# Six of the weight ring's units become three double-width tiles, loaded from weights laid out in pairs of experts

## The chip, the cores and the metric

One core of one Trainium2 chip runs the whole program in one launch. The metric is the device time of that launch in microseconds. Before the change it is 1020.64 us (median of 3 runs, 1019.25 to 1020.99).

## The reference

Two transformer layers run one after the other on 256 tokens of width 1024. The first has a mixer (differential attention and gated linear attention), a cross attention to a memory, and a mixture of experts; the second has three attention branches, one of them a cross attention to the same kind of memory. All is float32. The part that matters here is the mixture of experts: 32 experts, two per token, each with three matrices.

```python
def expert_block(args):                       # N_EXPERTS = 32, D_MODEL = 1024, D_EXPERT = 512
    xb, e = args
    hid = jax.nn.silu(xb @ w_gate[e]) * (xb @ w_up[e])     # w_gate, w_up: 32 x 1024 x 512
    return hid @ w_down[e]                                 # w_down:        32 x 512 x 1024
...
kv = rmsnorm(mem, g_mem) @ w_mem_kv           # second layer: 1024 x 1024, the memory's keys and values
```

## The kernel before

The mixture of experts works on groups of four experts (q = 0 to 7), each expert with 32 token slots, so that four experts fill the 128 columns of TensorE. `experts(q)` gathers the tokens, multiplies by gate and up (L1065), forms the hidden rows, multiplies by down (L1090) and adds the result to the tokens (L1101, L1108).

Every weight is loaded once. A "unit" is 8 KB on each of 128 partitions, 1024 KB, and one unit holds half of one matrix of one expert: 192 units in all, 24 per q, asked for four at a time by `weights(4)` (one for each of the four experts). Units live in a ring of 20 slots. The string `ORDER = "222222uuuu11111uuu3u"` says, request by request, from which pool the slot comes: `2` from `ring2` (tag w2, 6 slots), `u` from `utp` (tag ut, 8 slots shared with other tiles), `1` from `ring1` (w1, 5 slots), `3` from `ring3` (w3, one slot). `unit()` (L89) takes the letter at `st["n"]` and steps on. A slot is written again when the instructions that read what it held are done; the wait for it stands on the load itself.

All weight loads are issued by SyncE's queue (SP), which is in order: a load that waits holds back all behind it. Loads take one of eight completion semaphores in turn, so a load also waits for the one eight places before it. The first 20 requests are chained in program order (`chained()`, L1000); later a scheduler places them.

Beside the experts stands work for the second layer, as filler: after q = 4 `mem2_k` (L1179) and after q = 5 `mem2_v` multiply the normalised memory by `w_mem_kv_2`. Each asks for two units through `w_units` (L146, its load is L156), which calls the same `unit()`; so these two requests take the next two letters of the ring. `mem2_k` is the 121st and 122nd request, letters 1 and 2 of the string's seventh turn. Each of its units is split chunk by chunk into a high and a low part, on ScalarE (`whf`, L327) and VectorE (`wlf`, L328), with two buffers of each, and each chunk feeds 12 matmuls (L363, L365, L366).

`pack()` on the host prepares the inputs; `woven` puts the rows of an expert's matrix in the order in which a partition wants them, so that a unit is 1024 KB in one piece in HBM.

Of the kernel before, what the change touches and what calls it, by code (L numbers as in the profile page):

```python
# [8 lines left out]
F32 = mybir.dt.float32  # L9
# [7 lines left out]
P = 128  # L17
# [51 lines left out]
def tile_layers(ctx: ExitStack, tc: tile.TileContext, A, out, dbg=None, upto=99):  # L69
    nc = tc.nc  # L70
    V, S, PE, G, SP = nc.vector, nc.scalar, nc.tensor, nc.gpsimd, nc.sync
    R1, R2, R3, UT, K2A, K2B = 5, 6, 1, 8, 26, 31
# [12 lines left out]
    st = {"ring2": None, "n": 0, "floor": 10 ** 9}  # L85

    ORDER = "222222uuuu11111uuu3u"

    def unit(dt=F32):  # L89

        if st["ring2"] is None:
            return ring1.tile([P, 2048], dt, tag="w1", name="w1", bufs=R1)
        r = ORDER[st["n"] % len(ORDER)]
        st["n"] += 1
        if r == "u":
            return ut((P, 2048), dt)
        if r == "1":
            return ring1.tile([P, 2048], dt, tag="w1", name="w1", bufs=R1)
        if r == "2":
            return st["ring2"].tile([P, 2048], dt, tag="w2", name="w2", bufs=R2)  # L100
        return st["ring3"].tile([P, 2048], dt, tag="w3", name="w3", bufs=R3)

    def pad(pool, nbytes):

        G.memset(pool.tile([P, nbytes // 4], F32, name="pad")[:, :1], 0.0)
# [7 lines left out]
    def tiny(n, dt=F32):  # L113
        return small.tile([P, n], dt, tag=f"t{n}", name=f"t{n}", bufs=8 if n < 32 else 3)

    def k2(shape=(P, 512), dt=F32):
        return st["k2"].tile(list(shape), dt, tag="k2", name="k2")

    def ut(shape=(P, 2048), dt=F32, name="ut"):
        return utp.tile(list(shape), dt, tag="ut", name=name, bufs=UT)  # L120
# [25 lines left out]
    def w_units(W, c0, n, k0, nd, dmas=1, before=None):  # L146

        us = []
        for k in range(k0, k0 + nd, 4):
            u = unit()  # L150
            v = u[:, :4 * n].rearrange("p (d n) -> p d n", d=4)
            c = 4 // dmas
            for i in range(0, 4, c):
                if before:
                    before(k + i, c)
                SP.dma_start(v[:, i:i + c], W[(k + i) * P:(k + i + c) * P, c0:c0 + n].rearrange("(d p) n -> p d n", p=P))  # L156
            us.append(v)
        return us
# [12 lines left out]
    def load_T(t, src):  # L171
        return lambda d, n: SP.dma_start(t[:, d:d + n], src[:, d * T:(d + n) * T].rearrange("p (d t) -> p d t", d=n))

    us = w_units(A["w_in"], 0, 512, 0, 8, 2, load_T(xT, A["xT"]))
# [525 lines left out]
    for tt in range(2):  # L700
# [7 lines left out]
        for hp in range(2):  # L708
            for cc in range(2):
                c = 2 * tt + cc  # L710
# [31 lines left out]
    for tt in range(2):  # L742
        t = k2()
# [75 lines left out]
    for hp in range(2):  # L819
        for tt in range(2):  # L820
# [9 lines left out]
            for hh in range(2):  # L830
                j = 2 * hp + hh
# [9 lines left out]
    for hd in range(4):  # L841
# [4 lines left out]
        p = wspf.tile([P, 2, T], F32, tag="whf", name="p", bufs=2)  # L846
# [151 lines left out]
    loads, loaded = [], []  # L998

    def chained():  # L1000

        return tc.issue_after(st["dma"].ins) if 0 < len(loaded) < len(ORDER) else nullcontext()

    def add_gu(q, k):
        def go(g, j):
            u = unit().rearrange("p (d n) -> p d n", d=4)
            with chained():
                st["dma"] = SP.dma_start(u, A[g][4 * q + j, 4 * k * P:(4 * k + 4) * P, :].rearrange("(p d) n -> p d n", p=P))
            return [u]
        loads.extend([lambda g=g, j=j: go(g, j) for g in ("w_e_gate", "w_e_up") for j in range(4)])  # L1010

    def add_dn(q, k, fine):
        W = A["w_e_down"]

        def go(j):
            u = unit().rearrange("p (c n) -> p c n", c=2)
            with chained():
                st["dma"] = SP.dma_start(u, W[4 * q + j, 2 * k * P:2 * (k + 1) * P, :].rearrange("(p c) n -> p c n", p=P))
            return [u]

        def go_fine():
            us = [unit().rearrange("p (c n) -> p c n", c=2) for _ in range(4)]
            for b, c0, c1 in ((0, 0, 2), (1, 0, 1), (1, 1, 2)):
                for j in range(4):
                    SP.dma_start(us[j][:, c0:c1, b * 512:(b + 1) * 512],
                                 W[4 * q + j, 2 * k * P:2 * (k + 1) * P, b * 512:(b + 1) * 512]
                                 .rearrange("(p c) n -> p c n", p=P)[:, c0:c1])
            return us
        loads.extend([go_fine] if fine else [lambda j=j: go(j) for j in range(4)])

    for q in range(8):
        for k in range(2):
            add_gu(q, k)
        for k in range(2):
            add_dn(q, k, fine=q == 7 and k == 1)
# [222 lines left out]
    for tt in range(2):  # L1258
# [5 lines left out]
        w = tiny(8)  # L1264
# [8 lines left out]
    for tt in range(2):  # L1273
        nk = (tt + 1) * P
        acc = accs[tt]
        for p0 in range(0, 4, 4 // (tt + 1)):
            n = 4 // (tt + 1)
# [6 lines left out]
            for r in range(2):  # L1284
                rl = k2((P, n, nk))
                S.activation(rl, pss[r], AF.Relu)
                for p in range(n):
                    g = 2 * (p0 + p) + r
# [154 lines left out]
    for tt in range(2):  # L1443
        m4, s4, nb, r4 = tiny(4), tiny(4), tiny(4), tiny(4)
        for f in range(2):
# [7 lines left out]
            for hh in range(2):  # L1453
                j = 2 * f + hh
                S.activation(x[:, hh], ps[:, hh], AF.Exp, bias=nb[:, j:j + 1], scale=isc, accum_out=s4[:, j:j + 1])
            V.reciprocal(r4[:, c2], s4[:, c2])
            for hh in range(2):
                j = 2 * f + hh
# [3 lines left out]
    for hd in range(4):  # L1462
# [4 lines left out]
        p = k2((P, 2, T))  # L1467
# [35 lines left out]
def pack(inputs):  # L1503
    f = {k: np.asarray(v) for k, v in inputs.items()}
    c, m = shape_constants()
    row = lambda *n: [f[k].reshape(-1) for k in n]
    vecs = np.concatenate(row("norm_mix", "norm_cross", "norm_mem", "norm_ffn", "g_in_2", "g_mem_2", "b_merge_2",
                              "da_q_norm", "da_q_norm", "da_k_norm", "da_k_norm", "da_out_norm", "gla_out_norm",
                              "cross_q_norm", "cross_k_norm")).reshape(NVEC, P)

    woven = lambda w, c: w.reshape(32, -1, c, P, w.shape[-1]).transpose(0, 1, 3, 2, 4).reshape(w.shape)
    chunks = lambda w: np.ascontiguousarray(w.reshape(8, P, -1).transpose(1, 0, 2).reshape(P, -1))
    feature = lambda x: x.T.reshape(8, P, T).transpose(1, 0, 2).reshape(P, -1)
    a = {
        "x": f["x"][0], "mem": f["mem"][0], "mem_2": f["mem_2"][0],
        "xT": feature(f["x"][0]), "memT": feature(f["mem"][0]), "vecT": vecs.T, "cst": c, "cstm": m,
        "lam": np.concatenate([f[k] for k in ("lambda_q1", "lambda_k1", "lambda_q2", "lambda_k2")], 0),
        "gw": np.tile(np.pad(f["gla_gate_w"][0], ((0, 16), (0, 0))), (4, 1)), "gb": f["gla_gate_b"],
        "w_gr": chunks(np.pad(f["w_in"][0][:, 3072:3088], ((0, 0), (0, 16)))),
        "w_rt": chunks(np.concatenate([f["w_group"][0], np.zeros((D, 4), np.float32), f["w_expert"][0]], 1)),  # L1520
        "b_rt": np.concatenate([f["b_group"][0], np.full(4, -3e38, np.float32), f["b_expert"][0]])[None],
        "g_final": f["g_final_2"][None],
    }
    for k in ("w_in", "w_o", "w_cq", "w_ckv", "w_co", "w_e_gate", "w_e_up", "w_e_down", "w_in_2", "w_mem_kv_2",
              "w_up_moba_2", "w_up_dsa_2", "w_up_cross_2", "w_out_2"):
        a[k] = f[k][0]
    for k, c in (("w_e_gate", 4), ("w_e_up", 4), ("w_e_down", 2)):
        a[k] = woven(a[k], c)
    return {k: np.ascontiguousarray(v) for k, v in a.items()}


_INS = ("x", "mem", "mem_2", "xT", "memT", "vecT", "cst", "cstm", "lam", "gw", "gb", "w_gr", "w_rt", "b_rt", "g_final",
        "w_in", "w_o", "w_cq", "w_ckv", "w_co", "w_e_gate", "w_e_up", "w_e_down", "w_in_2", "w_mem_kv_2",
        "w_up_moba_2", "w_up_dsa_2", "w_up_cross_2", "w_out_2")


# [14 lines left out]
```

## Time and profile before

| | us |
|---|---|
| median of 3 runs | 1020.64 |
| the profiled execution, its own time | 1020.82 |
| its span, on which all times below are read | 1019.2 |
| TensorE busy | 905.2 (89%) |
| VectorE, ScalarE busy | 445.4, 357.8 |
| data read from HBM | 292.98 MB |
| chain that ended last: TensorE, DMA | 46%, 40% |

The times of the rows are microseconds from the span's start. The span is cut into 40 slices of 25.5 us on the page; the mixture of experts lies in slices 11 to 28, counted from 1 (about 255 to 712 us). GB/s is what the core's 16 DMA engines moved. In a row of time, a bracket holds the idle time before the instruction and what ended it. A wait of the queue is read as the time between two issues.

### The profile page before, as it was taken

To read this page: it belongs to the slowest core of one execution; us is meant where nothing else is said; L and a number is where in the kernel's file an instruction comes from. 1 tells how busy PE (TensorE), PEld (TensorE's weight loads), DVE (VectorE), ACT (ScalarE), POOL (GpSimd) and SP (SyncE) were. 2 spreads that over 40 slices of the span, in tenths; PEclk is the share of its full clock that TensorE was granted. 3 is DMA by queue.
4 is the path that set the end of the run, shared out by engine and by line. 5 is a ranking of instruction groups with operands and counts; after the bars stand their busy time and mean duration, and the time that the engine had idled before them with its cause. 6 is when DMAs were issued, how large, how long until landed. Compare 5 with 4: busy or idle time off the path is not lost.

```text
span 1019.2 us, 14146 instructions
## 1 busy us (share of the span) xinstructions
PE 905.2 (89%) x5611; PEld 603.0 (59%) x5611; DVE 445.4 (44%) x999; ACT 357.8 (35%) x687; POOL 48.0 (5%) x180
## 2 busy tenths in 40 slices
PE   6999999999978869678797897778999999999996
PEld 6787788877423313114152251113878788999994
DVE  4596664535311202003030130103997967646465
ACT  5675765444101001002020020003645656554443
POOL 1101423101000001000000000000000000000000
PEclk9999999999989999899899999979999999999998
DMA  9853354698899999999999999999645352446531
GB/s 328 317 165 125 125 172 159 212 388 316 358 420 426 426 427 426 429 426 427 426 422 426 424 426 426 428 427 338 209 149 180 105 186 84 143 153 200 187 124 42
DMA packets 77029, 294.98 MB, mean 289 GB/s; under 512 B 5280, under 2 KB 8096, under 8 KB 52768
## 3 DMA queue, kind: packets, MB, share of 16 engines
q1 hardware_dynamic: 76672, 293.48, 74.0%
q8 instruction: 45, 0.74, 0.3%
q10 hardware_dynamic: 288, 0.57, 0.1%
q14 instruction: 24, 0.20, 0.1%
HBM read 292.98 MB, written 1.05 MB: 288 GB/s over the span
## 4 chain that ended last, share of the span: by engine, by line
PE 46%; DMA 40%; DVE 6%; ACT 4%; POOL 2%; issue 1%; DVEq 0%; SPq 0%; ACTq 0%; POOLq 0%
DMA ut<-w_e_up 15%; DMA w<-w_e_up 10%; DMA ut<-w_e_down 7%; PE mm L357 6%; PE mm L363 6%; PE mm L365 6%; PE mm L366 6%; PE mm L358 6%; PE mm L356 6%; DMA w<-w_e_down 5%; DVE wlm L328 2%; DMA ut<-w_mem_kv 2%; PE mm L1065 2%; ACT whm L327 1%; PE mm L1090 1%
## 5 line engine op out<-in xcount | busy, mean ns | idle before, releaser
L328 DVE TENSOR_TENSOR wlm<-w,whm 128x1024 fp32r<-128x1024 f32 (+3 forms) x144 | 168.5, 1173 | 110.3 <-ACT whm L327 108.7
L327 ACT ACTIVATE whm<-w 128x1024 fp32r<-128x1024 f32 (+3 forms) x144 | 145.6, 1014 | 145.1 <-PE mm L365 69.8
L1065 PE MATMUL mm<-w,xg 128*32 128x512 f32 x616 | 148.0, 661 | 33.3 <-DMA w<-w_e_gate 18.5
L363 PE MATMUL mm<-uh,whm 128*128 128x256 f32 x448 | 129.1, 288 | 6.6 <-ACT whm L327 6.6
L365 PE MATMUL mm<-ul,whm 128*128 128x256 f32 x448 | 128.3, 286 | 0.0
L1065 PE MATMUL mm<-ut,xg 128*32 128x512 f32 x408 | 108.0, 643 | 22.8 <-DMA ut<-w_e_up 15.4
L366 PE MATMUL mm<-uh,wlm 128*128 128x256 f32 x448 | 128.0, 286 | 0.0
L357 PE MATMUL mm<-wlm,uh 128*128 128x512 f32 (+2 forms) x288 | 111.4, 387 | 4.0 <-DVE wlm L328 4.0
L356 PE MATMUL mm<-whm,uh 128*128 128x512 f32 (+2 forms) x288 | 110.7, 388 | 0.4 <-ACT uh L291 0.2
L358 PE MATMUL mm<-whm,ul 128*128 128x512 f32 (+2 forms) x288 | 110.7, 385 | 0.0
L1090 PE MATMUL mm<-w,hT 128*32 128x512 f32 x320 | 83.8, 599 | 12.4 <-DMA w<-w_e_down 9.7
L363 PEld LDWEIGHTS mm<-uh,whm 128*128 128x128 f32 x448 | 86.9, 194 | 7.4 <-ACT whm L327 6.6
L1065 PEld LDWEIGHTS mm<-w,xg 128*32 128x32 f32 x616 | 32.0, 119 | 93.6 <-issue 44.5
L365 PEld LDWEIGHTS mm<-ul,whm 128*128 128x128 f32 x448 | 87.0, 194 | 0.6 <-issue 0.2
L366 PEld LDWEIGHTS mm<-uh,wlm 128*128 128x128 f32 x448 | 86.9, 194 | 0.1
L1065 PEld LDWEIGHTS mm<-ut,xg 128*32 128x32 f32 x408 | 24.8, 116 | 75.9 <-issue 30.8
L1090 PE MATMUL mm<-ut,hT 128*32 128x512 f32 x192 | 58.8, 599 | 7.4 <-DMA ut<-w_e_down 5.7
L357 PEld LDWEIGHTS mm<-wlm,uh 128*128 128x128 f32 x288 | 54.2, 188 | 17.2 <-DVE wlm L328 7.4
L356 PEld LDWEIGHTS mm<-whm,uh 128*128 128x128 f32 x288 | 53.8, 188 | 11.0 <-ACT whm L327 0.9
L358 PEld LDWEIGHTS mm<-whm,ul 128*128 128x128 f32 x288 | 54.1, 188 | 10.1 <-issue 0.3
L1097 DVE COPY eo<-mm 128x256 f32<-128x256 f32 x16 | 6.8, 424 | 119.1 <-ACT eo L1096 119.1
L1053 DVE SCALAR_TENSOR_TENSOR mt<-mt,mm 128x512 f32<-128x512 f32 x8 | 5.5, 687 | 119.2 <-ACT mt L1052 119.2
(349 smaller groups left out, 1261.4 us busy)
## 6 DMA issues: line engine op xcount, KB each, us to landing
w<-w_in SPq DMA_DIRECT2D x42, 1024.0 KB, 4.9
w<-w_e_gate SPq DMA_DIRECT2D x42, 1024.0 KB, 19.6
w<-w_e_down SPq DMA_DIRECT2D x37, 1024.0 KB, 19.6
w<-w_e_up SPq DMA_DIRECT2D x35, 1024.0 KB, 19.6
ut<-w_e_up SPq DMA_DIRECT2D x29, 1024.0 KB, 19.5
ut<-w_e_down SPq DMA_DIRECT2D x23, 1024.0 KB, 19.6
ut<-w_e_gate SPq DMA_DIRECT2D x22, 1024.0 KB, 19.5
w<-w_ckv SPq DMA_DIRECT2D x8, 1024.0 KB, 5.1
```

The source lines that it names most:

```text
L327: S.activation(wh, src, AF.Copy)
L328: st["wl"] = V.tensor_tensor(wl, src, wh.bitcast(F32), op=OP.subtract)
L356: PE.matmul(o, uh[:, d, sl], wh[:, dd], start=d == d0, stop=False)
L357: PE.matmul(o, uh[:, d, sl], wl[:, dd], start=False, stop=False)
L358: PE.matmul(o, ul[:, d, sl], wh[:, dd], start=False, stop=d == d1)
L363: PE.matmul(o, wh[:, dd, sl], uh[:, d], start=d == d0 and f % 2 == 0, stop=False, skip_group_check=True)
L365: PE.matmul(o, wh[:, dd, sl], ul[:, d], start=False, stop=False, skip_group_check=True)
L366: PE.matmul(o, wl[:, dd, sl], uh[:, d], start=False, stop=d == d1, skip_group_check=True)
L1053: V.scalar_tensor_tensor(t, t, 1.0, gp, op0=OP.add, op1=OP.mult)
L1065: PE.matmul(ps[32 * j:32 * j + 32], xg[:, d, 32 * j:32 * j + 32], us[j][:, dd], start=d == 0, stop=d == 7, tile_position=(0, 32 * j))
L1090: PE.matmul(dn[b][32 * j:32 * j + 32], hT[:, c, 32 * j:32 * j + 32], us[j][:, cc, b * 512:(b + 1) * 512], start=c == 0, stop=c == 3, tile_ ...
L1097: V.tensor_copy(o[:, 256:], dn[b][:, 256:])
```

## The change

`unit_pair()` is new: where the next two letters are both `2`, it takes one tile of 16 KB per partition (tag w2, 3 of them in the same room) and gives its two halves; elsewhere it gives two single units. The host lays the same half matrix of two neighbouring experts side by side: a row of 4096 floats per partition, 16 KB, of which the first 8 KB belong to one expert and the second to the next. A double tile is loaded by one transfer of 2048 KB; single units are loaded by one transfer each, of half of every such row. The very last group of loads (`go_fine`) and the overflow path read the old arrays. The branch for letter `2` in `unit()` is gone; a single request that meets that letter takes the last line, `ring3`.

```diff
         if r == "1":
             return ring1.tile([P, 2048], dt, tag="w1", name="w1", bufs=R1)
-        if r == "2":
-            return st["ring2"].tile([P, 2048], dt, tag="w2", name="w2", bufs=R2)
         return st["ring3"].tile([P, 2048], dt, tag="w3", name="w3", bufs=R3)
+
+    def unit_pair():
+
+        if ORDER[st["n"] % len(ORDER)] + ORDER[(st["n"] + 1) % len(ORDER)] == "22":
+            st["n"] += 2
+            t = st["ring2"].tile([P, 4096], F32, tag="w2", name="w2", bufs=R2 // 2)
+            return t, [t[:, :2048], t[:, 2048:]]
+        return None, [unit(), unit()]
...
+    def go(src):
+        t, us = unit_pair()
+        for u, w in [(t, src)] if t is not None else zip(us, (src[:, :2048], src[:, 2048:])):
+            with chained():
+                st["dma"] = SP.dma_start(u, w)
+        return us
+
     def add_gu(q, k):
-        def go(g, j):
-            u = unit().rearrange("p (d n) -> p d n", d=4)
-            with chained():
-                st["dma"] = SP.dma_start(u, A[g][4 * q + j, 4 * k * P:(4 * k + 4) * P, :].rearrange("(p d) n -> p d n", p=P))
-            return [u]
-        loads.extend([lambda g=g, j=j: go(g, j) for g in ("w_e_gate", "w_e_up") for j in range(4)])
+        loads.extend([lambda g=g, j=j: [u.rearrange("p (d n) -> p d n", d=4) for u in go(A[g][2 * q + j, k])]
+                      for g in ("w_gate_2", "w_up_2") for j in range(2)])
...
+
+        a[k.replace("_e", "") + "_2"] = a[k].reshape(16, 2, 2, P, 2048).transpose(0, 2, 3, 1, 4).reshape(16, 2, P, 4096)
```

SP's queue at the end of q = 4, before the change. `w2_3981` and `w2_3983` are the two units of `mem2_k`, `w3_3940` is a unit of q = 4's down matrices, and what follows is q = 5's gate.

```order
L1018 DMA w3_3940<-w_e_down 128x2048
L1018 DMA ut_3942<-w_e_down 128x2048
L156 DMA w2_3981<-w_mem_kv_2 128x4x512
L156 DMA w2_3983<-w_mem_kv_2 128x4x512
L1008 DMA w2_4117<-w_e_gate 128x2048
L1008 DMA w2_4119<-w_e_gate 128x2048
L1008 DMA w2_4121<-w_e_gate 128x2048
L1008 DMA w2_4123<-w_e_gate 128x2048
```

The same place of SP's queue in the changed kernel:

```order
L1014 DMA w3_3904<-w_down_2 128x2048
L1014 DMA ut_3905<-w_down_2 128x2048
L1014 DMA w2_4081<-w_gate_2 128x4096
L162 DMA w3_3945<-w_mem_kv_2 128x4x512
L1014 DMA w2_4083<-w_gate_2 128x4096
L1014 DMA w1_4143<-w_gate_2 128x2048
L162 DMA w3_3947<-w_mem_kv_2 128x4x512
L1014 DMA w1_4144<-w_gate_2 128x2048
L1014 DMA w1_4147<-w_gate_2 128x2048
```

The memory's two units now carry the tag w3, as the unit of q = 4 two places ahead does, and they stand behind and between loads of q = 5, with three units of q = 5 between them. They are the only single units of the program that meet letter `2`.

ScalarE's order around `mem2_k`, before (`eo` is the end of q = 4, `whf` the split of the memory's weights, `xg` the gather for q = 6, `mt` the hidden rows of q = 5):

```order
L1096 ACTIVATE eo_3969<-mm_3911 128x256
L327 ACTIVATE whf_3985<-w2_3981 128x512
L327 ACTIVATE whf_4001<-w2_3981 128x512
L327 ACTIVATE whf_4017<-w2_3981 128x512
L327 ACTIVATE whf_4033<-w2_3981 128x512
L327 ACTIVATE whf_4049<-w2_3983 128x512
```

and in the changed kernel:

```order
L1100 ACTIVATE eo_3933<-mm_3875 128x256
L968 ACTIVATE xg_4128<-sm_4129,vec_86 128x128
L968 ACTIVATE xg_4128<-sm_4136,vec_86 128x128
L968 ACTIVATE xg_4128<-sm_4191,vec_86 128x128
L333 ACTIVATE whf_3949<-w3_3945 128x512
L333 ACTIVATE whf_3965<-w3_3945 128x512
L968 ACTIVATE xg_4128<-sm_4198,vec_86 128x128
L333 ACTIVATE whf_3981<-w3_3945 128x512
```

The gather for q = 6 moved ahead of the split; on TensorE it moved likewise, and the first two matmuls of q = 5's gate units moved in between. Elsewhere the three engines keep their order but for two matmuls that changed places.

SP's queue where the ring turns for the first time, before (`w2_2816` is the 21st request, the first that takes a used slot of the ring):

```order
L1018 DMA w3_2665<-w_e_down 128x2048
L1018 DMA ut_2667<-w_e_down 128x2048
L1018 DMA w2_2816<-w_e_down 128x2048
L1018 DMA w2_2818<-w_e_down 128x2048
L1018 DMA w2_2820<-w_e_down 128x2048
L1018 DMA w2_2822<-w_e_down 128x2048
```

and in the changed kernel:

```order
L1014 DMA w3_2659<-w_down_2 128x2048
L1014 DMA ut_2660<-w_down_2 128x2048
L1014 DMA w2_2810<-w_down_2 128x4096
L1014 DMA w2_2812<-w_down_2 128x4096
L1014 DMA w2_2848<-w_gate_2 128x4096
```

Two loads stand where four stood, each behind the readers of both units that the slot held. There are 29 such loads in the program, 3 of them in the first 20 requests; 130 single units remain, 116 of them behind the first 20 requests.

## Rows read from the trace of the kernel before

**Rows 1.** The page: DMA share (tenths) and GB/s in 40 slices

```profile
DMA  9853354698899999999999999999645352446531
GB/s 328 317 165 125 125 172 159 212 388 316 358 420 426 426 427 426 429 426 427 426 422 426 424 426 426 428 427 338 209 149 180 105 186 84 143 153 200 187 124 42
```

**Rows 2.** Engines by stretch; after the engines: PEclk, DMA share, GB/s

```profile
255.00:262.00 7.00, 6.63 (x56) 3.14 (x56) 2.79 (x16) 0.73 (x2) 0.00 (x0) 1.00 0.62 260
262.00:264.00 2.00, 2.00 (x18) 1.64 (x15) 0.35 (x1) 0.05 (x1) 0.00 (x0) 1.00 0.68 143
264.00:266.00 2.00, 2.00 (x20) 0.77 (x22) 0.68 (x2) 0.68 (x2) 0.00 (x0) 1.00 0.93 393
266.00:268.00 2.00, 2.00 (x21) 0.48 (x13) 0.00 (x0) 0.00 (x0) 0.00 (x0) 1.00 1.06 442
420.00:460.00 40.00, 29.27 (x132) 7.01 (x132) 2.52 (x6) 1.58 (x3) 0.00 (x0) 0.91 1.01 427
```

**Rows 3.** Chain of waits in order of time: start, us, what

```profile
257.52 0.89 PE mm L1065 x2
...
263.71 12.09 DMA w<-w_e_down
...
564.55 19.78 DMA ut<-w_mem_kv
...
584.39 19.56 DMA ut<-w_e_up
...
698.85 1.48 PE mm L1090 x9
```

**Rows 4.** The page: DMA issues, count, KB each, us to landing

```profile
w<-w_e_gate SPq DMA_DIRECT2D x42, 1024.0 KB, 19.6
...
w<-w_co SPq DMA_DIRECT2D x4, 1024.0 KB, 5.0
```

**Rows 5.** SP's queue in time, end of q = 4 and after

```profile
493.16 0.33 SPq L1018 DMA_DIRECT2D w<-w_e_down  x1
495.63 0.33 SPq L1018 DMA_DIRECT2D ut<-w_e_down  x1
...
535.10 12.75 SPq L1008 DMA_DIRECT2D ut<-w_e_up  x3
```

**Rows 6.** TensorE in time at the end of q = 4

```profile
512.81 1.90 PE L1090 MATMUL mm<-w,hT 128*32 128x512 f32 x4 [0.54 <-DMA w<-w_e_down]
515.25 0.64 PE L1090 MATMUL mm<-ut,hT 128*32 128x512 f32 x3 [0.53 <-DMA ut<-w_e_down]
...
516.99 1.88 PE L1090 MATMUL mm<-ut,hT 128*32 128x512 f32 x4
...
522.14 0.68 PE L363 MATMUL mm<-uh,whf 128*128 128x256 f32 x1
```

**Rows 7.** ScalarE in time at the end of q = 4

```profile
518.11 0.38 ACT L1096 ACTIVATE eo<-mm 128x256 f32<-128x256 f32 x1 [16.74 <-PE mm L1090]
```

**Rows 8.** VectorE in time at the end of q = 4

```profile
522.23 1.28 DVE L1108 TENSOR_TENSOR h<-sm,h 128x512 f32<-128x512 f32 x2
...
526.21 0.69 DVE L328 TENSOR_TENSOR wlf<-w,whf 128x512 fp32r<-128x512 f32 x1 [0.81 <-ACT whf L327]
```

**Rows 9.** SP's queue in time, first fill and first turn of the ring

```profile
198.14 0.34 SPq L1008 DMA_DIRECT2D w<-w_e_gate  x1
...
251.54 0.33 SPq L1018 DMA_DIRECT2D ut<-w_e_down  x1
261.67 0.33 SPq L1018 DMA_DIRECT2D w<-w_e_down  x1
...
262.45 1.17 SPq L1018 DMA_DIRECT2D w<-w_e_down  x2
```

**Rows 10.** TensorE in time, the end of q = 5's filler and after

```profile
533.98 0.28 PE L366 MATMUL mm<-uh,wlf 128*128 128x256 f32 x1
...
549.84 3.63 PE L1065 MATMUL mm<-w,xg 128*32 128x512 f32 x28 [1.45 <-DMA w<-w_e_gate]
```

More of the change, by code (lines that the diff above doesn't have):

```diff
@@ L1002, in chained @@
         return tc.issue_after(st["dma"].ins) if 0 < len(loaded) < len(ORDER) else nullcontext()
-    def add_gu(q, k):
-        def go(g, j):
-            u = unit().rearrange("p (d n) -> p d n", d=4)
-            with chained():
-                st["dma"] = SP.dma_start(u, A[g][4 * q + j, 4 * k * P:(4 * k + 4) * P, :].rearrange("(p d) n -> p d n", p=P))
-            return [u]
-        loads.extend([lambda g=g, j=j: go(g, j) for g in ("w_e_gate", "w_e_up") for j in range(4)])
+    def go(src):
[4 more added lines that the diff above has]
+        return us
+    def add_gu(q, k):
+        loads.extend([lambda g=g, j=j: [u.rearrange("p (d n) -> p d n", d=4) for u in go(A[g][2 * q + j, k])]
+                      for g in ("w_gate_2", "w_up_2") for j in range(2)])
     def add_dn(q, k, fine):
         W = A["w_e_down"]
[L1015 to L1019, printed above, removed]
         def go_fine():
-            us = [unit().rearrange("p (c n) -> p c n", c=2) for _ in range(4)]
+            us = [u.rearrange("p (c n) -> p c n", c=2) for _ in range(2) for u in unit_pair()[1]]
             for b, c0, c1 in ((0, 0, 2), (1, 0, 1), (1, 1, 2)):
@@ L1028, in go_fine @@
             return us
-        loads.extend([go_fine] if fine else [lambda j=j: go(j) for j in range(4)])
+        loads.extend([go_fine] if fine else [lambda j=j: [u.rearrange("p (c n) -> p c n", c=2) for u in go(A["w_down_2"][2 * q + j, k])]
+                                             for j in range(2)])
     for q in range(8):
@@ L1528, in pack @@
         a[k] = woven(a[k], c)
+        a[k.replace("_e", "") + "_2"] = a[k].reshape(16, 2, 2, P, 2048).transpose(0, 2, 3, 1, 4).reshape(16, 2, P, 4096)
     return {k: np.ascontiguousarray(v) for k, v in a.items()}
 _INS = ("x", "mem", "mem_2", "xT", "memT", "vecT", "cst", "cstm", "lam", "gw", "gb", "w_gr", "w_rt", "b_rt", "g_final",
-        "w_in", "w_o", "w_cq", "w_ckv", "w_co", "w_e_gate", "w_e_up", "w_e_down", "w_in_2", "w_mem_kv_2",
-        "w_up_moba_2", "w_up_dsa_2", "w_up_cross_2", "w_out_2")
+        "w_in", "w_o", "w_cq", "w_ckv", "w_co", "w_e_gate", "w_e_up", "w_e_down", "w_gate_2", "w_up_2", "w_down_2", "w_in_2",
+        "w_mem_kv_2", "w_up_moba_2", "w_up_dsa_2", "w_up_cross_2", "w_out_2")
 def kernel(**inputs):
```

## The prediction

> **What bounds the kernel now.** I read the slices of the page first. From slice 12 on, for sixteen slices, the 16 DMA engines are busy throughout and move 420 to 429 GB/s; the last twelve slices have 42 to 209 [rows 1]. This is the mixture of experts, and TensorE is not what holds it: in the 40 us from 420 it is busy for 29 [rows 2]. The chain of waits says the same: from 263.71 on it is almost only DMA, in links of mostly 19.56 us, up to the last down group at 698.85 [rows 3]. A link is one load from issue to landing, 19.6 us against 5.0 for a load that finds the queue empty [rows 4]. Eight loads are in flight, so a unit lands every 19.56/8 = 2.445 us (1.0486 MB in that time is 428.9 GB/s). In this stage every microsecond in which the DMA engines have nothing to do comes out at the end, and what TensorE does costs nothing unless it holds back a load.
>
> **Part 1, the wide loads themselves.** 29 loads of 2048 KB replace 58 of 1024; 26 of them lie behind the first turn of the ring, where DMA bounds. What is a row worth that is 16 KB long instead of 8? The link that holds `mem2_v`'s two units took 19.78 against 19.56 for one without [rows 3]. Those units come in rows of 2 KB, 32 rows per engine and unit instead of 8, so 48 more rows per engine cost 0.22 us, 4.6 ns a row. A wide load saves 8 rows per engine, 37 ns; 26 of them save 1.0 us. The row's own cost may not fall if the engines cut 16 KB in pieces: then 0. On the other side, the quickest stretch shown is 442 GB/s [rows 2]; wide loads at that rate instead of 428.9 would save 3% of 26 x 4.89 us, 3.8 us. I take -1.0, the value of the nearest row, with 0 and -3.8 as ends.
>
> **Part 2, the single units.** Their rows stay 8 KB long but now lie 16 KB apart. Before shows no such load. The nearest are the memory's units, 2 KB rows 4 KB apart, and 0.11 us a unit is all they cost over the others. I have put that down to the number of rows, so 0 here. If all of it came from the gaps between rows instead, 116 units would cost 12.8 us, and part 1 nothing.
>
> The Trainium skill ("DMA: Bandwidth & Descriptors", Latency and other measured facts) tells of copies that lose rate when the pitch of a partition's rows is a large power of two, 207 GB/s of 214 at 512 KiB and half at 4 MiB. It lists no pitch as small as 16 KiB. By its 3% on 116 units the sum would be some 9 us higher, as an estimate; the rows of the memory's units speak against that for a pitch of 4 KB.
>
> **Part 3, the first turn of the ring.** The 21st load waits for TensorE to read the first units, from 251.54 to 261.67, and the next three follow at 262.45 and after [rows 9]; meanwhile the DMA engines run dry (260 GB/s from 255 to 262 [rows 2]). The wide load holds both units, so it goes when the second is free. I take 262.45, when its own load goes in before: 0.8 us later. Everything behind is bound by DMA, so it costs 0.8 (0.3 if the second unit is free sooner than its load was issued, which stood behind another).
>
> Elsewhere a wide load waits for two units that the same group of four reads side by side, and TensorE trails DMA by less than the ring's 20 slots, so this costs nothing; at the first fill (198 to 255) slots wait for the cross attention, and TensorE reaches the first expert only at 257 [rows 3, 9]. There a few microseconds of DMA are covered. If that cover were gone it would show at 261.67.
>
> **Part 4, the memory's units in the one-slot pool.** This is not in the description of the change. `mem2_k`'s two requests meet letter `2` as single units and so fall into `w3`. I call them A and B. A needs the slot of q = 4's unit `w3_3904`, B needs A's. SP's queue is in order: behind A wait half of q = 5's first gate group and all else, behind B the rest of q = 5.
>
> A first. In the trace of before the w3 unit is issued at 493.16, and the unit behind it at 495.63 [rows 5]; they land at 512.81 and 515.25, where TensorE takes them [rows 6]. The w3 unit's last matmul stands one before the end of its group, four at a time in 0.43 us, and the group ends at 516.99 + 1.88 = 518.9; the first half's `eo` could start at 518.11 [rows 7], and the w3 unit's last matmul retires next to that. So A is issued at about 518.25. What is in flight then? Behind the w3 unit only its neighbour, landed at 515.25, and the first wide load, which would land at 515.25 + 4.89 = 520.14. The queue has run dry but for that.
>
> What does a dry queue cost? The first turn of the ring shows it. The 21st load is issued at 261.67, the 24th at 263.71, and that one lands 12.09 later, at 275.80 [rows 3, 9]. Four units at 2.445 are 9.78, so landings run as if the first had begun 275.80 - 9.78 - 261.67 = 4.35 us after its issue. GB/s agree: 143 and 393 in the four microseconds after 262, then 442 [rows 2]. So A costs 518.25 + 4.35 - 520.14 = 2.5 us. If only the 5.0 us of an empty queue counted [rows 4], it would be 518.25 + 5.0 - 520.14 - 2.445 = 0.7; if the slot came free only with the group's end (518.9 and a wait of 0.3), 3.4.
>
> B next. A lands between 518.25 + 5.0 = 523.2 and 518.25 + 4.35 + 2.445 = 525.05; say 524. ScalarE has three copies of the gather ahead of the split, and these wait for VectorE's additions, done at 523.5 [rows 8], so they barely matter. In before, from the first matmul of the filler at 522.14 [rows 6] to the end of the fourth chunk's low part, 526.21 + 0.69 = 526.90 [rows 8], is 4.76 us: chunks 3 and 4 wait for the two buffers, which matmuls free. First split at 524, matmuls from 524.8, slot free at 529.5, B issued at 529.7. In flight then: the second wide load and one unit, landing at 525.05 + 7.34 = 532.4. Cost 529.7 + 4.35 - 532.4 = 1.7 us; between 0 (A early, or an empty queue's price) and 2.9 (A late).
>
> Does TensorE lose too? In before it does all eight chunks without a pause, to 534, and has caught up with DMA by 549.84 [rows 10]. Now it waits for B, to some 535, doing half a gate group meanwhile, ends the filler near 541, and is then less behind than DMA is: no cost. `w3`'s next unit, in q = 5's down group, is asked for 11 units after B, so B's slot is free by then. `mem2_v` meets the letters `u`, as before.
>
> **Sum**, against the profiled execution (1020.82 us, 1019.2 of it the span): -1.0 + 0 + 0.8 + 2.5 + 1.7 = +4.0, so 1024.8. That execution is 0.18 above the median of the runs, so for a median I say 1024.6. Its own range: stalls of 0.7 + 0 to 3.4 + 2.9, start 0.3 to 0.8, rows -1.0 to 0, which is 0 to +7.1, or 1020.6 to 1027.7.
>
> **Rivals.**
>
> 1. The stalls are covered. The dry queue costs only what an empty one shows (0.7 and 0), the rest is +0.8 and -1.0: +0.5, 1021.1. For it: in before SP stalls for most of the 12.75 us from 535.10, just behind this filler, and the rate of no slice there falls under 422 [rows 1, 5]. Against: then five and more units were in flight, now two or three.
>
> 2. The wide loads speed the stream. At 442 GB/s they save 3.8 us, and with the stalls at their low end (0.7 + 0, and 0.8 at the start) the time is 1020.6 - 3.8 + 1.5 = 1018.3. It decides where a pair lands in under 4.75 us rather than 4.89 if the stalls are small, and under 4.62 if they are as I forecast. Against: 442 stands in a stretch of 2 us only, and thirteen slices hold 426 to 429 [rows 1, 2].
>
> 3. The fixed time of a load counts in full. A load alone takes 5.0 us of which 2.445 move data; if each load paid the other 2.55 one after the other, 26 fewer would save 66 us: 954.6. Landings every 2.445 us with eight in flight leave no room for it. The Trainium skill ("DMA: Bandwidth & Descriptors", Measured) speaks for it in form: it gives 341 GB/s for 1 MB and 425 for 16 MB and advises larger batches. Here units of 1 MB run at 428.9, so the trace does not agree where loads overlap.
>
> 4. The pitch costs (part 2 at its bound): +12.8 + 0.8 + 4.2, 1038.4.
>
> **How the numbers follow.** Forecast 0.60, rival 1 0.22, rival 2 0.10, rival 3 0.02, rival 4 0.06. No change is within 0.2%, 1018.6 to 1022.7, about what a measurement of this kernel can tell. Of the forecast's 0.60 some 0.05 falls there, with rival 1: 0.27. Faster is rivals 2 and 3, 0.12; slower 0.55 + 0.06 = 0.61. The range takes the forecast and rival 1 and a little on either side, 1019.2 to 1028.5.
>
> **What would show it.** A right: SP's queue has a wait of A on TensorE's down matmuls (L1094) near 518, and one of B on VectorE's split near 529; GB/s fall well below 420 twice between 517 and 533. Part 1: loads land 4.85 us behind the one before where they are wide, and the slices otherwise still read 426 to 430. Part 3: the 21st load's issue near 262.5. Wrong: slices that read 435 or more (rival 2), slices all below 420 (rival 4), or no dip at q = 5 (rival 1). I would also be wrong if the stalls are longer because B comes so late that TensorE, not DMA, sets q = 5's end.

## The result, and the profile after

The changed kernel takes 1026.3 us (median of 4 runs, 1025.8 to 1028.11), the kernel before beside it 1020.81: a ratio of 1.0068 [1.0055, 1.0081], +5.5 us. The forecast was +4.0, at 1024.6, and the range held the time. The profiled execution has 1025.8 us, 1024.1 of it the span.

The first thing to read is the slices of the page after, beside [rows 1].

```profile
DMA  9854354698899999999979999999645252445531
GB/s 334 308 164 127 121 188 143 243 376 312 348 421 429 427 429 425 429 430 426 427 321 403 423 428 430 427 428 378 226 130 199 87 189 97 131 160 195 194 124 42
```

All but two of the sixteen slices in which DMA bounds read as before, 421 to 430. Slice 21 has 321 and slice 22 has 403: the loss lies between 512 and 563 us. Cut in windows (columns as in [rows 2]), that stretch of the changed kernel reads:

```profile
514.00:516.00 2.00, 1.44 (x13) 0.43 (x16) 0.00 (x0) 0.00 (x0) 0.00 (x0) 1.00 1.02 438
516.00:518.00 2.00, 2.00 (x12) 0.44 (x4) 0.04 (x1) 0.38 (x1) 0.00 (x0) 1.00 0.54 229
518.00:520.00 2.00, 1.86 (x5) 0.84 (x5) 1.21 (x3) 0.38 (x1) 0.00 (x0) 1.00 0.52 135
520.00:522.00 2.00, 2.00 (x6) 0.80 (x6) 1.67 (x3) 0.00 (x0) 0.00 (x0) 1.00 1.19 470
528.00:530.00 2.00, 2.00 (x18) 2.00 (x19) 0.38 (x1) 0.63 (x1) 0.00 (x0) 1.00 0.62 258
530.00:532.00 2.00, 2.00 (x19) 2.00 (x19) 1.00 (x2) 0.63 (x1) 0.00 (x0) 1.00 0.00 0
532.00:534.00 2.00, 2.00 (x20) 1.43 (x22) 0.00 (x0) 0.00 (x0) 0.00 (x0) 1.00 0.29 89
534.00:536.00 2.00, 2.00 (x24) 0.64 (x20) 0.00 (x0) 0.00 (x0) 0.00 (x0) 1.00 1.05 408
558.00:561.00 3.00, 1.79 (x6) 0.14 (x2) 0.00 (x0) 0.00 (x0) 0.00 (x0) 1.00 0.80 238
```

There are three dips. What each lacks against 428.9 GB/s, divided by 428.9, is the time lost: (199.9 + 293.9) x 2 / 428.9 = 2.3 us in the first, (170.9 + 428.9 + 339.9) x 2 / 428.9 = 4.4 in the second, 190.9 x 3 / 428.9 = 1.3 in the third. From 530 to 532 nothing moves at all. SP's queue over the same time (start, us, line, tile and source, count) shows who holds the loads:

```profile
495.08 0.33 SPq L1014 DMA_DIRECT2D ut<-w_down  x1
497.49 0.33 SPq L1014 DMA_DIRECT2D w<-w_gate  x1
517.56 0.38 SPq L162 DMA_DIRECT2D w<-w_mem_kv  x1
517.99 0.97 SPq L1014 DMA_DIRECT2D w<-w_gate  x2
531.77 0.38 SPq L162 DMA_DIRECT2D w<-w_mem_kv  x1
532.20 1.62 SPq L1014 DMA_DIRECT2D w<-w_gate  x3
533.86 1.88 SPq L1014 DMA_DIRECT2D ut<-w_up  x4
536.67 0.33 SPq L1014 DMA_DIRECT2D w<-w_up  x1
```

These answer to [rows 5]. A, the first unit of `mem2_k`, is issued at 517.56 and B at 531.77; between the wide load at 497.49 and A the queue issues nothing for 20 us, and between the loads at 517.99 and B nothing for 13. What it waits for (the waits of SP's queue from 515 to 532: total us, times, longest) is for B the split on VectorE, for A the down group's matmuls:

```profile
SPq L162 <- DVE wlf L334: 9.2, 1, 9.2
SPq L162 <- PE mm L1094: 5.3, 1, 5.3
```

Ahead of these waits stands another: A waits 14.4 us and B 3.6 us for the unit that holds the slot to land there at all.

The chain of waits ends with the last down group's matmuls at 703.97, against 698.85 [rows 3], so by the end of the experts the changed kernel is 5.1 us late; the two profiled executions differ by 5.0:

```profile
408.06 26.79 DMA ut<-w_up
...
474.14 20.88 DMA w<-w_up
495.08 19.56 DMA ut<-w_down
...
703.97 1.96 PE mm L1094 x12
```

### The profile page after: what moved, and what is told of

Its sections match the earlier page's. It is cut to its first block, busy times and chain, and to the rows that moved or that the text cites. A ratio compares the mean times of both kernels' runs of the same rounds, so it can differ in the third digit from the quotient of the medians.

```text
span 1024.1 us, 14101 instructions
## 1 busy us (share of the span) xinstructions
PE 901.0 (88%) x5611; PEld 601.6 (59%) x5611; DVE 445.1 (43%) x999; ACT 357.6 (35%) x687; POOL 47.8 (5%) x180
## 4 chain that ended last, share of the span: by engine, by line
PE 49%; DMA 36%; DVE 7%; ACT 4%; POOL 2%; issue 2%; SPq 1%; DVEq 0%; ACTq 0%; POOLq 0%
DMA ut<-w_up 11%; DMA w<-w_down 7%; PE mm L363 7%; DMA ut<-w_down 6%; PE mm L364 6%; PE mm L369 6%; PE mm L371 6%; PE mm L362 6%; PE mm L372 6%; DMA w<-w_gate 4%; DMA ut<-w_gate 3%; PE mm L1069 2%; DMA w<-w_up 2%; DVE wlm L334 2%; DMA ut<-w_e_down 1%
## 5 line engine op out<-in xcount | busy, mean ns | idle before, releaser
L1069 PE MATMUL mm<-w,xg 128*32 128x512 f32 x616 | 145.6, 700 | 35.9 <-DMA w<-w_up 18.2
L1069 PE MATMUL mm<-ut,xg 128*32 128x512 f32 x408 | 108.9, 651 | 27.9 <-DMA ut<-w_up 19.7
L1094 PE MATMUL mm<-w,hT 128*32 128x512 f32 x320 | 80.0, 609 | 14.0 <-DMA w<-w_down 11.1
L1069 PEld LDWEIGHTS mm<-w,xg 128*32 128x32 f32 x616 | 31.2, 124 | 95.0 <-issue 48.0
L1069 PEld LDWEIGHTS mm<-ut,xg 128*32 128x32 f32 x408 | 25.0, 117 | 85.2 <-DMA ut<-w_up 35.8
L1094 PE MATMUL mm<-ut,hT 128*32 128x512 f32 x192 | 56.7, 598 | 6.4 <-DMA ut<-w_down 4.4
```

Source lines behind the costliest of these rows:

```text
L1069: PE.matmul(ps[32 * j:32 * j + 32], xg[:, d, 32 * j:32 * j + 32], us[j][:, dd], start=d == 0, stop=d == 7, tile_position=(0, 32 * j))
L1094: PE.matmul(dn[b][32 * j:32 * j + 32], hT[:, c, 32 * j:32 * j + 32], us[j][:, cc, b * 512:(b + 1) * 512], start=c == 0, stop=c == 3, tile_ ...
```

## The experiments

Each kernel was timed in five rounds; kernels of one group ran on one chip with the kernel before. That kernel's medians were 1020.82 in the first group, 1019.86 in the second and 1019.90 in the third.

**Group 1: are the memory's units the cause, and all of it?** In the changed kernel, the two units share one wide tile:

```
-        for k in range(k0, k0 + nd, 4):
-            u = unit()
+        two = unit_pair()[1] if st["ring2"] is not None else None
+        for i, k in enumerate(range(k0, k0 + nd, 4)):
+            u = two[i] if two else unit()
```

> The changed kernel, with the memory's two units asked for as a pair, so that they take the two halves of a wide w2 tile and none of them ring3. Theory (the loss is the two waits of A and B in the one-slot pool, and the wide loads bring 1 to 2 us): the dips of GB/s between 516 and 534 are gone and the time is 1019.0 to 1020.0. Rival 1 (the halved rows of the single units cost): it stays above 1024. Rival 2 (a wide load that waits for both its units costs): it stays above 1023, with a later first turn and no dip.

Measured: 1018.59 us, ratio to before 0.9974 [0.9954, 0.9993], 0.4 us under the range expected. All three dips are gone; the page of this kernel:

```profile
GB/s 332 314 166 125 125 167 165 215 374 314 347 422 428 427 430 425 430 429 426 427 425 426 424 428 428 429 427 359 211 151 177 105 187 84 144 154 199 188 125 42
```

No slice from the 12th to the 27th is under 422. The rest of the change, wide loads and new arrays, does not slow the kernel.

The converse: the kernel before, with nothing changed but that these two units go to the one-slot pool (`unit(mem=True)` in `w_units`):

```
-        if r == "2":
+        if r == "2" and not mem:
```

> The kernel before, with one edit: the memory's two units take ring3 where they meet letter 2. No wide tile, old layout. Theory: two dips of GB/s around 517 and 530 as in the changed kernel, +6 to +8 us, 1027 to 1029. Rivals 1 and 2: the waits are covered by other loads in flight, 1020 to 1022.

Measured: 1027.77 us, 1.007 [1.0042, 1.0097]. Its SP queue has the same two holes, and its page the same two slices (311 and 403):

```profile
518.50 0.38 SPq L156 DMA_DIRECT2D w<-w_mem_kv  x1
...
532.73 0.38 SPq L156 DMA_DIRECT2D w<-w_mem_kv  x1
```

B again comes 14.2 us behind A. So the units' pool makes the loss without any wide tile, and the loss goes with it.

What is the single transfer worth? The first experiment's kernel, with each wide tile loaded by two transfers of 1024 KB:

```
-        for u, w in [(t, src)] if t is not None else zip(us, (src[:, :2048], src[:, 2048:])):
+        for u, w in zip(us, (src[:, :2048], src[:, 2048:])):
```

> e1 with each wide tile loaded by two transfers of 1024 KB instead of one of 2048; tiles, layout and the places of the memory's units as in e1. If the rows of 16 KB are what saves time (4.6 ns a row), it is 1.0 us slower than e1, 1020.5. If the row's length brings nothing, it is equal to e1. If each load pays a fixed time, it is many us slower.

Measured: 1019.77 us, 0.999 [0.9976, 1.0004]; 1.2 us over the same kernel with one transfer. And the layout alone: the changed kernel with the ring of single units back, so that every load of a unit is one row of 8 KB out of 16:

```
+        if r == "2":
+            return st["ring2"].tile([P, 2048], dt, tag="w2", name="w2", bufs=R2)
         return st["ring3"].tile([P, 2048], dt, tag="w3", name="w3", bufs=R3)
...
-        if ORDER[st["n"] % len(ORDER)] + ORDER[(st["n"] + 1) % len(ORDER)] == "22":
-            st["n"] += 2
-            t = st["ring2"].tile([P, 4096], F32, tag="w2", name="w2", bufs=R2 // 2)
-            return t, [t[:, :2048], t[:, 2048:]]
```

> The kernel before with the paired layout alone: every unit is a single tile and a single load of 8 KB rows that lie 16 KB apart; six w2 slots as before, so the memory's units stay in ring2. Theory: as before, 1020 to 1021.3. Rival 1 (the distance between rows costs, up to 0.11 us a unit): 1025 to 1039, with all slices of the experts below 425 GB/s.

Measured: 1019.11 us, 0.9982 [0.9966, 0.9998], 1.7 under the kernel before and 0.9 under the range expected. Its links, in the chain of waits, say that the layout costs nothing (start, us, what):

```profile
334.25 19.57 DMA ut<-w_up
353.88 19.55 DMA w<-w_up
...
494.00 20.75 DMA ut<-w_down
...
583.90 19.56 DMA ut<-w_up
```

Nor do they say that it gains anything: 19.55 to 19.57 is before's link. This experiment differs from the third only in that a pair is two tiles, not one, and 0.66 us in time; the traces show 0.79 of difference in the first turn (below).

**Group 2: where does the layout's 1.7 us come from, and what does B alone do?** The kernel before with the three paired arrays as further inputs that nothing reads:

```
+        a[k.replace("_e", "") + "_2"] = a[k].reshape(16, 2, 2, P, 2048).transpose(0, 2, 3, 1, 4).reshape(16, 2, P, 4096)
```

> The kernel before with the three paired arrays handed in and never read. e4 was 1.7 us under before, which the theory did not expect. If that comes from where the arrays stand in HBM or from the inputs' number: 1019.1. If it comes from reading rows that lie 16 KB apart, or was chance: 1020.8, and as wide a spread of runs as before.

Measured: 1019.81, 1.000 [0.999, 1.001]. And the first experiment's kernel with its single units read from the old arrays, in one piece (`old` are their rows in `w_e_gate`, `w_e_up`, `w_e_down`):

```
-        for u, w in [(t, src)] if t is not None else zip(us, (src[:, :2048], src[:, 2048:])):
+        for u, w in [(t, src)] if t is not None else zip(us, old):
```

> e1 with the single units read from the old arrays, 1024 KB in one piece; only the wide loads read the paired ones. If the paired layout of the single units is what saved in e4: 1.2 to 1.7 us slower than e1, 1019.8 to 1020.3, with a wider spread. If not: 1018.6 as e1.

Measured: 1018.48, 0.9988 [0.9978, 0.9997], against 1018.59 and 1018.83 of the kernel it changes. Neither the arrays nor the pitch moves the time, so the 1.7 us of the fourth experiment is not theirs. Of the 2.0 us between the two profiled executions 0.9 are there before the experts start: the first gather begins at 254.46 against 255.37, and in all twelve traces it lies between 254.46 and 256.04. The rest comes later, and in the chains single links are 1.2 to 1.5 us longer than their kind, at places that go with the kernel (474.14 and 474.20 in the two executions of the changed one). The kernel before, in its chain, has two:

```profile
435.38 20.99 DMA ut<-w_e_down
...
662.88 20.99 DMA ut<-w_e_up
```

The fourth experiment's execution has one of 20.75 and one of 19.94. They are loads that land late while GB/s hardly fall. In the kernel before, the unit due next after 665.27 lands 4.01 us later, at 669.28, instead of 2.445, and all behind it land late with it; its windows read:

```profile
666.00:668.00 2.00, 2.00 (x16) 0.42 (x8) 0.00 (x0) 0.00 (x0) 0.00 (x0) 0.77 1.01 418
668.00:670.00 2.00, 1.16 (x6) 0.14 (x2) 0.00 (x0) 0.00 (x0) 0.00 (x0) 1.00 1.01 426
```

Besides the loads, the page counts packets of instructions (number, MB, share):

```profile
q8 instruction: 45, 0.74, 0.3%
```

By the packets in the traces, each of the 24 landings between 276 and 690 us that come over 1 us late (those behind a dry queue left out) follows such a packet of 16 KB by 2.0 to 6.1 us; the two of the kernel before follow packets at 443.25 and 666.49. Every trace has 16 of them in that stretch, so most have no late landing behind them. That is an agreement in time; whether the packet is the cause, and why only some would have this effect, no run shows.

Then A in half of a wide tile and B in `w3`, where it waits for q = 4's down unit as A does in the changed kernel:

```
+        if one and one[0].shape[1] == 2048 and st["wide"]:
+            one[1] = st["ring3"].tile([P, 2048], F32, tag="w3", name="w3", bufs=R3)
```

> e1 with the memory's second unit in ring3: its first unit, A, takes half of a wide tile, and B waits for the slot that q = 4's down unit holds, as A does in the changed kernel. Nothing waits for the split any more. Theory (each dry queue has its own price, 2.3 us for the wait on the down group and 4.4 for the one on the split): one dip of GB/s near 518 and 1018.6 + 2.3 = 1020.9. Rival (only the wait on the split costs): 1018.6, as e1. Rival (the one-slot pool costs by its later use too): 1023 or more.

Measured: 1018.48, 0.9986 [0.9971, 1.0002]. My expectation missed by 2.4 us: there is a wait, but hardly a dip. In the windows of this kernel:

```profile
518.00:520.00 2.00, 1.87 (x6) 0.71 (x5) 1.11 (x3) 1.48 (x4) 0.00 (x0) 1.00 0.93 355
520.00:522.00 2.00, 2.00 (x7) 0.92 (x5) 1.83 (x4) 0.00 (x0) 0.00 (x0) 1.00 0.97 375
```

I had forgotten that A now stood in front, in flight. The unit behind the hole is issued at 517.69, as late as in the changed kernel; but the last load before it lands one unit later, at about 514.82 + 2.445 + 4.89 = 522.15, and 517.69 + 4.35 is 522.04. By the rule of the prediction the queue is not dry, and it was not: in the trace the load lands at 522.18 and the one behind the hole at 524.71, one unit later. One load more in flight pays for the whole wait.

**Group 3: A alone as it stands in the changed kernel.** A in `w3` with as many units in flight ahead of it as there, B in half of a wide tile and issued right behind it:

```
+        if one and st["wide"]:
+            one[0] = st["ring3"].tile([P, 2048], F32, tag="w3", name="w3", bufs=R3)
```

> The changed kernel with B taken out of ring3: A waits for the down unit's slot as before, with as many units in flight behind that (its neighbour and two more), B takes half of a wide tile and stands right behind A, so nothing waits for the split. Theory (a load has to be issued 4.35 us before the last one in flight lands, and A misses that by 2.3 us, B by 4.4): one dip near 518 and 2.3 us over e9, 1021. Rival (the split's wait is all of the loss): as e9. Rival (the first wait is all of it): as e10.

> e1 once more, on the chip of e8. All theories: no dip of GB/s at q = 5, and 1018.6 us as the first time.

> The changed kernel, on the chip of e8 and e9: both dips, 6 to 7 us over e9, 1025 to 1026.5.

Measured: 1020.42, 1.0011 [1.0002, 1.002], with A in `w3`; 1018.83, 0.9993 [0.9982, 1.0004], with neither (the first experiment again); 1026.2, 1.0072 [1.0059, 1.0085], for the changed kernel again. A alone costs 1.6 us where 2.3 were expected, A and B together 7.4 where 6 to 7 were, so B and what comes of it cost 5.8. The windows of the kernel with A alone:

```profile
516.00:518.00 2.00, 2.00 (x15) 0.59 (x11) 0.00 (x0) 0.00 (x0) 0.00 (x0) 1.00 0.83 352
518.00:520.00 2.00, 1.87 (x5) 0.49 (x3) 0.85 (x2) 0.77 (x2) 0.00 (x0) 1.00 0.19 71
520.00:522.00 2.00, 2.00 (x6) 0.95 (x5) 1.46 (x3) 0.00 (x0) 0.00 (x0) 1.00 1.04 400
...
558.00:561.00 3.00, 1.92 (x2) 0.18 (x2) 0.00 (x0) 0.00 (x0) 0.00 (x0) 0.57 1.02 431
```

They show the first dip, (76.9 + 357.9 + 28.9) x 2 / 428.9 = 2.2 us, and not the third. The changed kernel's second execution shows all three again: 0 GB/s from 530 to 532, 208 from 558 to 561.

With both units in a wide tile the kernel is 2.2 us under the kernel before in one group and 1.1 in the other, where the interval still holds 1. That is 0.1 to 0.2%, a gain that these runs show once and leave unclear once.

## Why the prediction was right, and where not

**Part 1, wide loads: -1.0 forecast, -1.2 measured** (first against third experiment, medians; their profiled executions, 1018.91 and 1018.59, stand the other way round, but in the third's the first gather begins 1.2 us earlier). The trace says the same. A link of the changed kernel that has three wide loads in it holds eleven units; eleven times 2.445 are 26.90 us, and it reads 26.79 (408.06, above; its like in the first experiment's kernel read 26.65 to 26.83): 0.11 for three loads, 37 ns each, what was taken from the memory's rows (the links' spread leaves 20 to 80 ns). Rival 2 has nothing for it: slices still read 421 to 430, though a wide load counts as one of eight in flight and so more bytes are under way. Rival 3 neither: the page gives a wide load 22 to 24 us to landing, and 26 fewer loads brought 1.2 us, not 66.

**Part 2, the pitch: 0 forecast, 0 measured** (the kernel that reads its single units from the old arrays, and links of 19.55 to 19.57 in the fourth). Rival 4 falls. The Trainium skill ("DMA: Bandwidth & Descriptors", Latency and other measured facts) tells of a loss at pitches from 512 KiB; at 16 KB the runs here show none.

**Part 3, first turn: +0.8 forecast.** The first gather starts at 255.37 in the kernel before and 255.10 in the changed one; the 21st unit's load is issued 6.30 us after it there [rows 9] and 7.09 here, at 262.19: +0.79. The third and fourth experiments have 7.08 and 6.29, and differ by 0.66 us in time.

**Part 4, A: +2.5 forecast**, 1.6 measured in time and 2.2 to 2.3 in the windows. A's neighbour reached TensorE 0.56 us earlier than before, at 514.69, and A was issued at 517.56, not 518.25; the rule gives 517.56 + 4.35 - (514.69 + 4.89) = 2.3. The mechanism holds: A waits for its slot, and the queue runs dry. The price of 4.35 us does not. "GB/s agree" misread its row: by 266, some 4.3 us behind the issue, the engines had moved (143 + 393) x 2 = 1072 KB [rows 2], a whole unit, where the rule has none. The same sum over the first turn of other traces gives 4.4 us (second experiment), 4.1 (unread arrays), 3.3 (fourth) and 2.4 (third), so 4.35 is one reading of one turn.

The landings in the changed kernel's trace speak for the price that the prediction set aside, 5.0 us from issue to landing. For the three loads from A on (us to landing: shortest, median, longest):

```profile
DMA to landing us min/median/max: 5.0/9.5/11.3
```

A is the 5.0, and the wide load ahead of it had landed at 519.50, so the landings lose 517.56 + 5.0 - 519.50 - 2.445 = 0.6 us there and not 2.3. The wide load itself landed late, behind one of the long links of group 2 (474.14, above); GB/s were down to 229 from 516 to 518, so many of its rows must have been in well before that. So the 2.3 of the windows agrees with a rule whose price other rows do not bear out, and that is partly luck.

**Part 4, B: +1.7 forecast, 4.4 in the window.** This is the term that was mis-sized. With the measured issues the rule gives 4.4: B issued at 531.77, the last load ahead of it due at 517.56 + 4.35 + 2.445 + 7.34 = 531.70, so 531.77 + 4.35 - 531.70. But here the 4.35 stands twice, with opposite signs, and says nothing of the price. In the trace the last load ahead of B landed at 529.88 (the 11.3 above); with 5.0 us from issue to landing, 531.77 + 5.0 - 2.445 - 529.88 is 4.4 as well. What made the term too small is the step before it, "so they barely matter", on ScalarE's gather copies. A lies there at 522.5. The split begins at 525.51, as the rows of TensorE, ScalarE and VectorE show (in brackets the idle time before, and what ended it):

```profile
521.98 3.73 PE L965 MATMUL sm<-Dm,xn 128*128 128x128 f32 x32
526.18 0.39 PE L369 MATMUL mm<-uh,whf 128*128 128x256 f32 x1 [0.47 <-ACT whf L333]
526.85 1.04 PE L1069 MATMUL mm<-w,xg 128*32 128x512 f32 x2
```

```profile
523.46 0.37 ACT L968 ACTIVATE xg<-sm,vec 128x128 f32<-128x128 f32 x1 [4.67 <-DVE xg L967]
525.25 0.37 ACT L968 ACTIVATE xg<-sm,vec 128x128 f32<-128x128 f32 x1 [0.52 <-DVE xg L967]
525.51 1.14 ACT L333 ACTIVATE whf<-w 128x512 fp32r<-128x512 f32 x2
530.39 0.63 ACT L333 ACTIVATE whf<-w 128x512 fp32r<-128x512 f32 x1 [0.81 <-PE mm L371]
```

```profile
526.36 1.29 DVE L334 TENSOR_TENSOR wlf<-w,whf 128x512 fp32r<-128x512 f32 x2
531.05 0.69 DVE L334 TENSOR_TENSOR wlf<-w,whf 128x512 fp32r<-128x512 f32 x1 [0.74 <-ACT whf L333]
```

I saw that the first copy waits for VectorE, and it did, to 523.46. But the gather of q = 6 had itself moved ahead of the filler on TensorE, 3.7 us of matmuls, and the last copy ahead of the split waits for it until 525.25. That is 1.5 us against my 524. From the split to the freed slot I had 5.5 us and it took 6.2 (531.05 + 0.69 = 531.74), with gate matmuls between the chunks' on TensorE. B came 2.1 us late; that A was issued 0.7 us early, and with it the loads ahead of B, added the rest. No run moved the gather alone; the second experiment, where B comes as late, has the same order on the three engines.

**What I had at nothing: the third dip, 1.3 us.** "TensorE no cost" is right as a sentence on TensorE, which waits for DMA there:

```profile
550.27 1.05 PE L1069 MATMUL mm<-ut,xg 128*32 128x512 f32 x2 [1.34 <-DMA ut<-w_up]
552.79 1.04 PE L1069 MATMUL mm<-ut,xg 128*32 128x512 f32 x2 [1.48 <-DMA ut<-w_up]
555.12 3.19 PE L1069 MATMUL mm<-ut,xg 128*32 128x512 f32 x25 [1.29 <-DMA ut<-w_up]
```

But I did not look at the order of the loads behind B. In the kernel before, SP's queue issues four loads for `ut` and then four of the gate:

```profile
513.99 6.76 SPq L1008 DMA_DIRECT2D ut<-w_e_up  x4
522.82 7.69 SPq L1008 DMA_DIRECT2D w<-w_e_gate  x4
```

In the changed kernel three gate loads stand directly behind B at 532.20 and the four for `ut` behind those, at 533.86. So the `ut` units land last, TensorE reads that group only from 555.12, when its fourth is there, and the load that needs one of their slots is held until 557.93 (the wait of SP's queue on the L1069 matmuls is 10.2 us): too late for the queue to stay full. The kernel with A alone has `ut` ahead of gate, as before, and no third dip. That the order is the cause is read from the two traces; no run changed the order alone.

**The sum.** The dips come to 8.0 us against 4.2 forecast; 7.4 were measured for them, third group. Wide loads and first turn add -1.2 and +0.7, so about +6.9 to +7.5 was to be expected where +5.5 and, in the third group, +6.3 were measured. For the profiled pair the late landings of group 2 are of that size: the kernel before carries two, 1.5 and 1.6 us, to the end of the experts. The changed kernel has one of 1.3 us ahead of A, most of which is gone behind the dry queue (the windows lose 2.3 us there, the landings 0.6), and one of 1.2 behind it. That the medians differ for the same reason is not shown. So the forecast came nearer to the time than its terms did: 3.8 us too little for B and the third dip, less some 1 to 2 us that no term of mine held. That is luck. Rival 1 had A's price as the landings show it (0.7 against 0.6), but a covered stall is refuted by a window with 0 GB/s.

## What to carry to other kernels

Where a queue of loads bounds the time, a wait on it costs nothing until the loads in flight run out: count what is in flight when the waiting load can go, and compare the time until the last of it lands with the time that a load into an empty queue takes. Read that time from more than one stall: one turn of one trace was not enough here. When a ring's slots are merged, ask of every other user of the ring where its request now lands; a request of another size that falls into a pool of one slot holds the whole in-order queue. And when the slot is freed by a chain over several engines, follow every engine's new order, not only the queue's: a gather that had moved ahead of the split is most of why B came 2.1 us late.

## What the runs showed of the hardware

A load that finds the queue (nearly) empty lands about 5.0 us after its issue, and not 19.56 as in the stream: A 4.97 and B 4.88 in the changed kernel, 4.9 to 5.3 in the four traces with such a stall. The next units then follow mostly 2.445 us apart, so a stall costs in landings what its load misses of that: 0.6 for A, 4.4 for B, nothing in the kernel with B alone in `w3`. The first turn of the ring shows more than that in some traces (6.8 us in the kernel before, 4.8 in the third experiment), which no run here explains. A transfer of 2048 KB in rows of 16 KB lands some 37 ns sooner than two of 1024 KB, with a spread of 20 to 80 in single links. Single loads land 1.1 to 1.7 us late while GB/s hardly fall, each of the 24 in twelve traces 2.0 to 6.1 us behind a packet of instructions; whether that packet is the cause is open. The lateness stays on all landings behind it, and most of it was gone behind a dry queue.
